# Sums for the down projection's left operands, made by VectorE and stored as seven operands

## The chip, the cores and the metric

One NeuronCore of one Trainium2 chip runs the whole program. The metric is the time of one execution on the device in microseconds (us). The engines are TensorE (PE in the profile, PEld its weight loads), VectorE (DVE), ScalarE (ACT), GpSimd (POOL) and SyncE (SP), whose queue issues nearly all transfers. Each engine runs its own instructions strictly in its own order and waits for others by semaphores.

## The reference

One layer of a decoder trunk on 1024 tokens of width 1024, in f32. The change concerns the feed-forward part alone:

```
h = rms_norm(x, ffn_norm_g)
x = x + (silu(h @ ffn_w_gate) * (h @ ffn_w_up)) @ ffn_w_down      # 1024 -> 2816 -> 1024
gate = sigmoid(rms_norm(x, ple_norm_g) @ ple_w_gate)
x = x + (p @ ple_w_proj) * gate
return rms_norm(x, final_norm_g)
```

Ahead of it stand the input projection, three token mixers and the output projection; nothing in them is changed.

## The kernel before

Matrices are kept transposed (features on the 128 partitions, tokens along the free dimension). Every f32 operand of a matmul is split in two: `split` (line 1037) makes the high part with a ScalarE cast (L1039) and the low part with a VectorE subtraction (`sub`, which all have line 267), and each product of 128x128 by 128x512 is three matmuls (high by high, high by low, low by high).

Both parts of the feed-forward use a fast 2x2 block multiplication: seven block products in place of eight, whose operands are sums and differences of the blocks a11 to a22 of the left matrix and b11 to b22 of the right one. In the order of use the seven left operands are: 5: a21+a22; 6: operand 5 minus a11; 3: a12 minus operand 6; 1: a11; 7: a11-a21; 4: a22; 2: a12.

**Feed-forward stage** (loop over `c`, 11 turns, lines 1278 to 1297). A turn computes 256 of the 2816 features by two objects of `Pair` (lines 1076 to 1134): n = 0 for the gate weights, n = 1 for the up weights. A Pair loads two 512 KB weight tiles (L1083), makes its sums on GpSimd (L1102 and L267), splits its seven operands and runs seven products of 12 matmuls (`prod`, L1050 to L1052) into three of the eight PSUM banks: `first` and `second` into bank a, `sixth` into b, `fifth` into c, and `rest` adds the other three. ScalarE copies partial results out of the banks. `quarters` (L1267, L1268) combines the banks and copies into four quarters on VectorE and GpSimd. For n = 0 these go into `act`, two tiles of 128x1024, and through Silu. For n = 1 they go into `up_` and are multiplied into `act` (L1295; quarters 1 and 3, which are a21 and a22 later, on GpSimd, the other two on VectorE), and both `act` tiles are written to `actd` in DRAM (L1297, 512 KB each). So a turn is 14 products, 168 matmuls.

**Down projection** (class `Down`, lines 1318 to 1351; loop at 1382 to 1408). It runs in four groups of three, three, three and two values of `c` (`DOWN`). A `Down` loads four 512 KB tiles, two of `actd` and two of `w_down` (L1326), and takes one tile `st` whose halves hold the running left sum `s` and right sum `t`. For each of the seven products in the order 5, 6, 3, 1, 7, 4, 2, `operands` makes the sums on GpSimd (four for the left: L1337 and three of L267; five for the right, L267), then splits left and right (ScalarE and VectorE). 36 matmuls per product in a group of three (L1406) go into the banks 0 to 3 or 4 to 7, and `drain` adds each bank to the result in SBUF on VectorE (L1316, L1369). The last group also loads and splits the next stage's weights (L1304 to L1308).

**What sets the order.** A planner (`Plan`) gives every tile one of 50 fixed slots of SBUF, 46 of them of 4 KB a partition, by program order and estimated times; a tile whose slot is still in use waits for its last reader. The compiler orders each engine's instructions by a simulated timeline, so that neighbouring parts of the program interleave; on the chip each engine then keeps that order, SyncE's queue included: a transfer that waits holds all transfers behind it.

Of the kernel before, what the change touches and what calls it, by code (L numbers as in the profile page):

```python
# [9 lines left out]
F32 = mybir.dt.float32  # L10
# [3 lines left out]
ALU = mybir.AluOpType  # L14
# [4 lines left out]
S = 1024  # L19
D = 1024  # L20
P = 128
# [5 lines left out]
MF = FF // P  # L27
# [191 lines left out]
def tile_block(ctx: ExitStack, tc: tile.TileContext, a: dict, out: bass.AP, plan: Plan):  # L219
    nc = tc.nc  # L220
# [7 lines left out]
    dram = ctx.enter_context(tc.tile_pool(name="dram", bufs=1, space=DRAM))  # L228
# [4 lines left out]
    def place(name, shape, dt):  # L233

        if dry:
            return big.tile(list(shape), dt, name=name, of=plan.add(4 * int(np.prod(shape[1:])), tc.clock))
        return big.tile(list(shape), dt, name=name, tag=f"s{plan.at[next(made)]}", bufs=1)

    def B(name, dt=F32, shape=(P, 1024)):
        return place(name, shape, dt)  # L240
# [7 lines left out]
    class Ring:  # L248


        def __init__(self, lo, hi):
            self.lo, self.hi, self.at = lo, hi, lo
# [10 lines left out]
    def f(ap):  # L263
        return ap.bitcast(F32)

    def sub(eng, o, i0, i1):
        return eng.tensor_tensor(out=o, in0=i0, in1=i1, op=ALU.subtract)  # L267
# [30 lines left out]
    def rstd_of(src, n, tag):  # L298

        r = SM(f"rs{tag}", src.shape)  # L300
        nc.gpsimd.tensor_scalar(out=r, in0=src, scalar1=1.0 / n, scalar2=EPS, op0=ALU.mult, op1=ALU.add)
        nc.gpsimd.tensor_tensor(out=r, in0=r, in1=mhalf[:, :src.shape[1]], op=ALU.pow)
        return r
# [413 lines left out]
    for t in range(NT):  # L717
# [4 lines left out]
        src = ps[:, :256].rearrange("p (g d) -> p g d", d=HD)  # L722
# [6 lines left out]
        if t > 2:  # L729
            pump(near, 1)  # L730
    nc.vector.tensor_tensor(out=gcmp, in0=gates.rearrange("p t (h b) -> p t h b", b=3)[:, :, :, 0],
                            in1=rowok.unsqueeze(2).to_broadcast([P, NT, H]), op=ALU.mult)
# [41 lines left out]
    for which in range(2):  # L774
# [4 lines left out]
        for u in range(2):  # L779
            for g in range(2):  # L780
                src = cv[g * 64:(g + 1) * 64, :].rearrange("p (n j) -> p j n", j=16)
                for q in range(2):
                    js = slice(q * 8, q * 8 + 8)
                    nc.vector.tensor_tensor(
                        out=X[q][u * 64:(u + 1) * 64, :, g * NCMP:(g + 1) * NCMP],
                        in0=src[:, js, u:u + NCMP],
                        in1=pos[g * 64:(g + 1) * 64, u, js].unsqueeze(2).to_broadcast([64, 8, NCMP]), op=ALU.add)
# [249 lines left out]
    def split(src):  # L1037
        o = B("op", F32R, (P, 2, 512))
        nc.scalar.copy(o[:, 0, :], src)  # L1039
        sub(nc.gpsimd if pool_lo[0] > 0 else nc.vector, o[:, 1, :], src, f(o[:, 0, :]))  # L1040
        pool_lo[0] -= 1
        return o

    def half(x, n):
        return x[:, n * 512:(n + 1) * 512]
# [91 lines left out]


    x1d = dram.tile([KT, P, S], F32, name="x1d")
    actd = dram.tile([MF, P, S], F32, name="actd")  # L1140
    xop, outs = {}, {}

    def out_half(m, hf, kts, first, last):
# [58 lines left out]
    for u in range(len(units) + LOOK):  # L1202
        ga = gb = iter(())
        if u < len(units):
            h, j = units[u]
# [25 lines left out]
    for m in range(KT):  # L1231
# [5 lines left out]
        if m == 4:  # L1237

            r = Right(raws[:4], [None] * 4)
# [3 lines left out]
    pairs = {}  # L1243
# [20 lines left out]
    def quarters(p, out):  # L1264

        rr = half(rbc1, 0), half(rbc1, 1)
        add = lambda eng, o, i0, i1: eng.tensor_tensor(out=o, in0=i0, in1=i1, op=ALU.add)  # L1267
        mult = lambda eng, o, i0, i1: eng.tensor_tensor(out=o, in0=i0, in1=i1, op=ALU.mult)  # L1268
        c11, c12, c21, c22 = out
        mult(nc.vector, c11, p.a, rr[0])  # L1270
        add(nc.vector, c12, p.c, p.p6)
        mult(nc.vector, c12, c12, rr[1])
        add(nc.vector, c21, p.b, p.p1)
        mult(nc.vector, c21, c21, rr[0])
        add(nc.gpsimd, c22, p.p67, p.p5)
        mult(nc.vector, c22, c22, rr[1])

    for c in range(MF // 2):
        for n in range(2):
            if (c, n) not in pairs:  # L1280
                pairs[c, n] = Pair(a["w_u" if n else "w_g"], 2 * c, r)
                pairs[c, n].first()
            p = pairs.pop((c, n))
            p.rest()
            if n == 0:
                act = [B("sg") for _ in range(2)]
                quarters(p, [half(g, i) for g in act for i in range(2)])
                for g in act:
                    nc.scalar.activation(g, g, AF.Silu)
            else:  # L1290
                up_ = [B("ws", F32, (P, 512)), p.p6, p.p1, p.p5]
                quarters(p, up_)
                for i, o in enumerate(up_):
                    g = half(act[i // 2], i % 2)
                    (nc.gpsimd if i in UPP else nc.vector).tensor_tensor(out=g, in0=o, in1=g, op=ALU.mult)  # L1295
                for i in range(2):
                    nc.sync.dma_start(out=actd[2 * c + i], in_=act[i])  # L1297


    wg = []  # L1300
# [17 lines left out]
    class Down:  # L1318


        def __init__(self, c):
            w = []
            for m in (2 * c, 2 * c + 1):
                for src in (actd[m], a["w_d"][m * P:(m + 1) * P, :]):
                    w.append(B("nat"))
                    nc.sync.dma_start(out=w[-1], in_=src)  # L1326
            self.a11, self.a21 = half(w[0], 0), half(w[0], 1)
            self.b11, self.b12 = half(w[1], 0), half(w[1], 1)
            self.a12, self.a22 = half(w[2], 0), half(w[2], 1)
            self.b21, self.b22 = half(w[3], 0), half(w[3], 1)  # L1330
            st = B("st", F32, (P, 2, 512))
            self.s, self.t = st[:, 0, :], st[:, 1, :]

        def operands(self, n):
            x = self
            if n == 5:
                nc.gpsimd.tensor_tensor(out=x.s, in0=x.a21, in1=x.a22, op=ALU.add)  # L1337
                sub(nc.gpsimd, x.t, x.b12, x.b11)
            if n == 6:
                sub(nc.gpsimd, x.s, x.s, x.a11)  # L1340
                sub(nc.gpsimd, x.t, x.b22, x.t)
            if n == 3:
                sub(nc.gpsimd, x.s, x.a12, x.s)
            if n == 7:
                sub(nc.gpsimd, x.a21, x.a11, x.a21)
                sub(nc.gpsimd, x.b12, x.b22, x.b12)
            if n == 4:
                sub(nc.gpsimd, x.t, x.b21, x.t)
            l, r = {5: (x.s, x.t), 6: (x.s, x.t), 3: (x.s, x.b22), 7: (x.a21, x.b12), 1: (x.a11, x.b11),
                    4: (x.a22, x.t), 2: (x.a12, x.b21)}[n]  # L1350
            return split(l), split(r)

    def acc(m, hf):
        return x2[hf][m % 4][:, m // 4, :]
# [27 lines left out]
    for q, cs in enumerate(DOWN):  # L1382
        ds = [Down(c) for c in cs]
        for n, g, start in ((5, 0, True), (6, 1, True), (3, 0, False), (1, 0, True), (7, 1, False), (4, 1, False),
                            (2, 0, False)):
            ops = [d.operands(n) for d in ds]
            if not x2:
                for hf in (1, 0):
                    x2.insert(0, [B("x2", F32, (P, 2, 512)) for _ in range(4)])
                    for m in range(KT):  # L1390
                        nc.sync.dma_start(out=acc(m, hf) if hf == 0 else x2[0][m % 4][:, m // 4, :],
                                          in_=half(x1d[m], hf))
# [9 lines left out]
            for t in range(4):  # L1402
                c = slice(t * P, (t + 1) * P)
# [26 lines left out]
    for i, t in enumerate(ORDER):  # L1430
        c = slice(t * P, (t + 1) * P)
        x, r3 = rows[i]
# [39 lines left out]
        r = rstd_of(ss, D, "r")  # L1472
# [64 lines left out]
def build(inputs):  # L1537
    import concourse.bacc as bacc

    nc = bacc.Bacc("TRN2", target_bir_lowering=False, num_devices=1)  # L1540
    arrays, aps = {}, {}
    for name, v in _layout({k: np.asarray(x) for k, x in inputs.items()}).items():
        v = np.ascontiguousarray(v)
        arrays[f"in_{name}"] = v
        aps[name] = nc.dram_tensor(f"in_{name}", v.shape, mybir.dt.from_np(v.dtype), kind="ExternalInput").ap()
    out = nc.dram_tensor("out_0", (S, D), F32, kind="ExternalOutput").ap()
    plan = Plan(SLOTS)
    tile_block(_Recorder(plan), aps, out, plan)
    plan.solve()
    with tile.TileContext(nc, schedule_with_timeline_sim=True) as tc:  # L1550
        tile_block(tc, aps, out, plan)
    return nc, arrays
# [8 lines left out]
```

## Time and profile before

| what | value |
|---|---|
| median of 3 runs | 1448.14 us (1444.1 to 1454.31) |
| the profiled execution's own time | 1443.36 us |
| its span, first to last instruction | 1441.6 us |
| busy: PE, DVE, ACT, POOL | 96%, 71%, 46%, 53% of the span |
| mean granted clock of TensorE | 0.988 of full speed |
| bytes moved | 118.36 MB, 82 GB/s |

The feed-forward stage lies from about 700 to 1077 us of the span and the down projection from about 1069 to 1316 us. A PE busy share is no measure of how full PE is, because matmuls overlap and the spans are modelled; the number of matmuls in a stretch is. In a timeline row the bracket says how long the engine was idle before, and who released it. "op" tiles are split operands, "nat" tiles are loaded as they are, "ws" and "st" hold sums, "cp" copies out of PSUM, "sg" is `act`.

### The profile page before, as it was taken

The page shows a single profiled execution, that of the slowest core. Times are in us where ns is not written, and L with a number is a line of the kernel's source. Part 1 is how long each engine was busy: PE and PEld are TensorE (multiplying, and loading weights), DVE is VectorE, ACT ScalarE, POOL GpSimd, SP SyncE. Part 2 cuts the span into 40 slices and gives each one's busy share as a digit, 9 for nine tenths or more (in the row PEclk, how much of TensorE's full clock was granted, in tenths as well). Part 3 has the DMA queues.
Part 4 walks back from the last instruction along what each step waited for, and adds up shares of the span by engine and source line. Part 5 has one row for each costly group of instructions (what it writes and reads, how often), then busy time and mean ns, then how long its engine had stood idle before and what let it go on. Part 6 is the DMA issues. An engine that isn't in the chain of part 4 may idle for free.

```text
span 1441.6 us, 19394 instructions
## 1 busy us (share of the span) xinstructions
PE 1387.6 (96%) x7080; PEld 1163.3 (81%) x7080; DVE 1028.8 (71%) x1738; ACT 665.6 (46%) x1290; POOL 765.6 (53%) x724
## 2 busy tenths in 40 slices
PE   8999999999999989999989999999997999999998
PEld 6898777889999978887768888888775877887886
DVE  3896548459999875678666666656679999987533
ACT  7321522348888874554333333333334343444632
POOL 3850433447887761045656665656687848514111
PEclk9999999999999999999999999999997999999999
DMA  9201012500000023521212222222282331321111
GB/s 350 74 16 49 16 57 80 165 0 5 9 5 5 5 92 126 181 73 45 88 73 75 86 88 88 88 73 88 65 298 93 132 139 38 131 74 62 66 41 44
DMA packets 40782, 118.36 MB, mean 82 GB/s; under 512 B 4532, under 2 KB 9326, under 8 KB 40686
## 3 DMA queue, kind: packets, MB, share of 16 engines
q1 hardware_dynamic: 40542, 117.11, 23.6%
q8 instruction: 55, 0.90, 0.3%
q14 instruction: 41, 0.34, 0.1%
q10 hardware_dynamic: 144, 0.01, 0.0%
HBM read 94.03 MB, written 23.08 MB: 81 GB/s over the span
## 4 chain that ended last, share of the span: by engine, by line
PE 52%; DVE 17%; POOL 12%; DMA 7%; issue 6%; ACT 5%; SPq 0%; POOLq 0%; DVEq 0%; ACTq 0%
DVE op L267 10%; PE banks L1406 6%; POOL ws L267 4%; PE banks L966 3%; PE banks L371 3%; PE banks L372 3%; PE banks L368 3%; ACT op L1039 3%; PE banks L1010 2%; PE banks L1011 2%; DMA nat<-in_w_u 2%; PE banks L906 2%; PE banks L1456 2%; PE banks L1457 2%; PE banks L1458 2%
## 5 line engine op out<-in xcount | busy, mean ns | idle before, releaser
L1050 PE MATMUL banks<-op 128*128 128x512 f32 x616 | 237.1, 393 | 8.2 <-ACT op L1039 4.2
L1051 PE MATMUL banks<-op 128*128 128x512 f32 x616 | 240.5, 391 | 0.7 <-DVE op L267 0.7
L1406 PE MATMUL banks<-op 128*128 128x512 f32 x924 | 222.6, 402 | 18.4 <-DVE x L1316 6.6
L1052 PE MATMUL banks<-op 128*128 128x512 f32 x616 | 238.9, 392 | 0.6 <-DVE op L267 0.4
L1406 PEld LDWEIGHTS banks<-op 128*128 128x128 f32 x924 | 178.1, 194 | 62.6 <-DVE x L1316 9.4
L267 DVE TENSOR_TENSOR op<-nat,op 128x512 fp32r<-128x512 f32 x174 | 162.0, 949 | 57.1 <-ACT op L1039 55.5
L1039 ACT CAST op<-nat 128x512 fp32r<-128x512 f32 x178 | 106.3, 620 | 179.1 <-DVE op L267 64.7
L1050 PEld LDWEIGHTS banks<-op 128*128 128x128 f32 x616 | 116.0, 188 | 37.3 <-ACT op L1039 5.1
L267 DVE TENSOR_TENSOR op<-ws,op 128x512 fp32r<-128x512 f32 x88 | 89.9, 1026 | 73.4 <-ACT op L1039 71.3
L1052 PEld LDWEIGHTS banks<-op 128*128 128x128 f32 x616 | 115.9, 188 | 27.3 <-DVE op L267 2.7
L1051 PEld LDWEIGHTS banks<-op 128*128 128x128 f32 x616 | 116.1, 188 | 24.9 <-DVE op L267 1.1
L921 POOL TENSOR_SCALAR p<-p,sums,gates 128x640 f32<-128x640 f32 (+7 forms) x128 | 100.4, 795 | 36.4 <-DVE sums L917 26.8
L1039 ACT CAST op<-ws 128x512 fp32r<-128x512 f32 x88 | 54.3, 620 | 101.1 <-POOL ws L267 74.7
L912 ACT ACTIVATE p<-p,mn 128x640 f32<-128x640 f32 (+7 forms) x128 | 94.8, 742 | 10.2 <-DVE mn L909 10.1
L368 PE MATMUL banks<-hT,whi 128*128 128x512 f32 x208 | 83.9, 404 | 6.8 <-ACT hT L324 6.2
L371 PE MATMUL banks<-hT,whi 128*128 128x512 f32 x208 | 83.4, 401 | 0.5 <-DVE hT L325 0.5
L372 PE MATMUL banks<-hT,wlo 128*128 128x512 f32 x208 | 82.0, 396 | 0.0
L267 DVE TENSOR_TENSOR op<-st,op 128x512 fp32r<-128x512 f32 x66 | 77.9, 1199 | 5.6 <-ACT op L1039 5.4
L1039 ACT CAST op<-st 128x512 fp32r<-128x512 f32 x66 | 39.8, 619 | 77.8 <-POOL st L267 48.3
L966 PE MATMUL banks<-cst,p 128*128 128x128 f32 x448 | 71.2, 274 | 2.0 <-DVE pt L267 1.0
L906 PE MATMUL banks<-k,qst 128*128 128x512 f32 (+2 forms) x192 | 68.0, 360 | 1.0 <-POOL qst L267 0.5
L267 DVE TENSOR_TENSOR pt<-banks,pt 128x512 fp32r<-128x512 f32 (+1 forms) x114 | 64.2, 571 | 5.9 <-ACT pt L977 4.9
(297 smaller groups left out, 3459.8 us busy)
## 6 DMA issues: line engine op xcount, KB each, us to landing
nat<-in_w_g SPq DMA_DIRECT2D x22, 512.0 KB, 3.3
nat<-in_w_u SPq DMA_DIRECT2D x22, 512.0 KB, 3.2
actd<-sg SPq DMA_DIRECT2D x22, 512.0 KB, 2.9
nat<-in_w_d SPq DMA_DIRECT2D x22, 512.0 KB, 5.3
nat<-actd SPq DMA_DIRECT2D x22, 512.0 KB, 4.6
nat<-in_w_t SPq DMA_DIRECT2D x13, 512.0 KB, 4.2
xT<-in_xT SPq DMA_DIRECT2D x16, 256.0 KB, 5.8
x<-in_x SPq DMA_DIRECT2D x8, 512.0 KB, 8.0
```

What stands on the lines that cost most here:

```text
L267: return eng.tensor_tensor(out=o, in0=i0, in1=i1, op=ALU.subtract)
L368: r = mm(o, hi[:, w], x[:, 0, :], start=kt == 0, stop=False)
L371: mm(o, hi[:, w], x[:, 1, :], start=False, stop=False)
L372: mm(o, lo_[:, w], x[:, 0, :], start=False, stop=kt == KT - 1)
L906: mark("pe", mm(ps[:, :max(w, 256)], q, kdup[br][g][:, k], start=True, stop=False))
L921: nc.gpsimd.tensor_scalar(out=ps_out[br][:, :n], in0=ps_out[br][:, :n], scalar1=sums[:, br:br + 1], scalar2=gates[:, qb, 3 * head(h) + 1 + ...
L966: nc.tensor.transpose(ps[:, (2 * m + e) * P:(2 * m + e + 1) * P], blk(e, kb, br, ka), ident)
L1039: nc.scalar.copy(o[:, 0, :], src)
L1050: mm(ps, w[:, 0, c], x[k][:, 0, :], start=start and k == 0, stop=False, skip_group_check=True)
L1051: mm(ps, w[:, 0, c], x[k][:, 1, :], start=False, stop=False, skip_group_check=True)
L1052: mm(ps, w[:, 1, c], x[k][:, 0, :], start=False, stop=k == 3, skip_group_check=True)
L1406: mm(groups[g][t], r[:, v, c], l[:, u, :], start=start and (i, u, v) == (0, 0, 0), stop=i == len(ops) - 1 and u == 1, skip_group_check=True)
```

## The change

`actd` becomes seven blocks of 128x512 for each `c`, one for each left operand in the order 5, 6, 3, 1, 7, 4, 2. In the feed-forward stage, behind the multiplications of n = 1, VectorE makes operands 5, 6, 3 and 7 in four instructions (5 and 6 in a new tile `sa`, 3 in the first tile of `up_`, 7 in place of a21), and five transfers write the seven blocks: 512 KB for 5 and 6, 256 KB for 3, 512 KB for 1 and 7, 256 KB for 4 and for 2.

`Down` loads the two weight tiles, operands 5 and 6 as one tile, and operand 2 into the half of `st` that `s` had; operands 3 and 1 are loaded when product 5's operands are made, 7 and 4 when product 3's are. GpSimd makes only the right sums.

In the last turn (c = 10) both Pairs are set up ahead: `first` of both, `sixth` of both, `fifth` of both, and only then the `rest` of each.

```
-    actd = dram.tile([MF, P, S], F32, name="actd")
+    actd = dram.tile([MF // 2, 7, P, 512], F32, name="actd")

     for c in range(MF // 2):
+        if c == MF // 2 - 1:
+            for n in range(2):
+                pairs[c, n] = Pair(a["w_u" if n else "w_g"], 2 * c, r)
+                pairs[c, n].first()
+            for n in range(2):
+                pairs[c, n].sixth()
+            for n in range(2):
+                pairs[c, n].fifth()
...
-                for i in range(2):
-                    nc.sync.dma_start(out=actd[2 * c + i], in_=act[i])
+                a11, a21, a12, a22 = (half(g, i) for g in act for i in range(2))
+                sa = B("sa", F32, (P, 2, 512))
+                s5, s6, s3 = sa[:, 0, :], sa[:, 1, :], up_[0]
+                nc.vector.tensor_tensor(out=s5, in0=a21, in1=a22, op=ALU.add)
+                sub(nc.vector, s6, s5, a11)
+                sub(nc.vector, s3, a12, s6)
+                sub(nc.vector, a21, a11, a21)
+                nc.sync.dma_start(out=actd[c, 0:2].rearrange("i p j -> p i j"), in_=sa)
+                nc.sync.dma_start(out=actd[c, 2], in_=s3)
+                nc.sync.dma_start(out=actd[c, 3:5].rearrange("i p j -> p i j"), in_=act[0].rearrange("p (i j) -> p i j", i=2))
+                nc.sync.dma_start(out=actd[c, 5], in_=a22)
+                nc.sync.dma_start(out=actd[c, 6], in_=a12)
...
         def __init__(self, c):
+            self.c, self.a = c, {}
             w = []
             for m in (2 * c, 2 * c + 1):
-                for src in (actd[m], a["w_d"][m * P:(m + 1) * P, :]):
-                    w.append(B("nat"))
-                    nc.sync.dma_start(out=w[-1], in_=src)
...
+                w.append(B("nat"))
+                nc.sync.dma_start(out=w[-1], in_=a["w_d"][m * P:(m + 1) * P, :])
+            self.b11, self.b12, self.b21, self.b22 = (half(x, i) for x in w for i in range(2))
+            self.load(5, 6)
             st = B("st", F32, (P, 2, 512))
-            self.s, self.t = st[:, 0, :], st[:, 1, :]
+            self.t, self.a[2] = st[:, 0, :], st[:, 1, :]
+            nc.sync.dma_start(out=self.a[2], in_=actd[c, 6])
+
+        def load(self, n0, n1):
+            i = (5, 6, 3, 1, 7, 4).index(n0)
+            w = B("nat", F32, (P, 2, 512))
+            nc.sync.dma_start(out=w, in_=actd[self.c, i:i + 2].rearrange("i p j -> p i j"))
+            self.a[n0], self.a[n1] = w[:, 0, :], w[:, 1, :]

             if n == 5:
-                nc.gpsimd.tensor_tensor(out=x.s, in0=x.a21, in1=x.a22, op=ALU.add)
+                x.load(3, 1)
                 sub(nc.gpsimd, x.t, x.b12, x.b11)
             if n == 6:
-                sub(nc.gpsimd, x.s, x.s, x.a11)
                 sub(nc.gpsimd, x.t, x.b22, x.t)
             if n == 3:
-                sub(nc.gpsimd, x.s, x.a12, x.s)
+                x.load(7, 4)
             if n == 7:
-                sub(nc.gpsimd, x.a21, x.a11, x.a21)
                 sub(nc.gpsimd, x.b12, x.b22, x.b12)
```

## Rows read from the trace of the kernel before

**Rows 1.** the page: span; busy us (share), instructions of each engine

```profile
span 1441.6 us, 19394 instructions
...
PE 1387.6 (96%) x7080; PEld 1163.3 (81%) x7080; DVE 1028.8 (71%) x1738; ACT 665.6 (46%) x1290; POOL 765.6 (53%) x724
```

**Rows 2.** stages: length, busy us (instructions) per engine, clock, DMA share, GB/s

```profile
738.00:1044.00 306.00, 305.17 (x1332) 250.24 (x1333) 192.96 (x222) 115.57 (x192) 184.68 (x126) 0.99 0.23 81
...
1069.00:1120.00 51.00, 38.59 (x132) 28.78 (x131) 47.33 (x48) 20.79 (x37) 40.40 (x24) 0.83 0.43 150
1120.00:1160.00 40.00, 38.45 (x169) 31.20 (x168) 37.60 (x43) 13.60 (x24) 37.56 (x24) 1.00 0.31 106
1160.00:1200.00 40.00, 40.00 (x178) 33.12 (x177) 39.12 (x53) 16.79 (x29) 20.40 (x14) 1.00 0.44 158
1200.00:1250.00 50.00, 47.68 (x203) 38.87 (x202) 48.23 (x62) 21.75 (x38) 28.54 (x18) 0.97 0.21 74
1250.00:1316.00 66.00, 63.86 (x277) 50.99 (x275) 61.83 (x77) 25.74 (x38) 30.39 (x19) 1.00 0.19 64
```

**Rows 3.** PE timeline, late feed-forward stage: start, us, instruction

```profile
1060.06 0.39 PE L1051 MATMUL banks<-op 128*128 128x512 f32 x1
...
1065.72 0.39 PE L1052 MATMUL banks<-op 128*128 128x512 f32 x1
```

**Rows 4.** PE timeline, start of the down projection

```profile
1090.00 6.51 PE L1406 MATMUL banks<-op 128*128 128x512 f32 x15 [3.38 <-DVE op L267]
...
1101.93 8.23 PE L1406 MATMUL banks<-op 128*128 128x512 f32 x26 [1.41 <-DVE x L1316]
```

**Rows 5.** VectorE timeline, start of the down projection

```profile
1081.44 1.77 DVE L267 TENSOR_TENSOR op<-nat,op 128x512 fp32r<-128x512 f32 x1
...
1101.80 2.97 DVE L267 TENSOR_TENSOR op<-nat,op 128x512 fp32r<-128x512 f32 x4
```

**Rows 6.** GpSimd timeline, the same stretch

```profile
1055.91 1.30 POOL L1134 TENSOR_TENSOR cp<-cp 128x512 f32<-128x512 f32 x1
...
1080.93 1.73 POOL L267 TENSOR_TENSOR st<-st,nat 128x512 f32<-128x512 f32 x1
```

**Rows 7.** groups of instructions, GpSimd, 1048 to 1316 us

```profile
L267 POOL TENSOR_TENSOR st<-nat,st 128x512 f32<-128x512 f32 x33 | 57.1, 1746 | 7.6 <-DVE op L267 7.6
...
L1337 POOL TENSOR_TENSOR st<-nat 128x512 f32<-128x512 f32 x11 | 18.4, 1675 | 10.5 <-PE banks L1406 6.4 <-DMA nat<-actd 4.1
```

**Rows 8.** chain of waits, 845 to 930 us: shares; start, us, what

```profile
by line: DMA nat<-in_w_u 14.6%; POOL ws L267 14.1%; DVE op L267 12.5%; POOL sg L1295 10.4%; issue 10.2%; ACT op L1039 8.1%; POOL cp L1133 5.8%; DVE sg L1268 5.6%; DMA nat<-in_w_g 3.7%; POOL cp L1134 3.4%; POOL cp L1267 3.1%; DVE cp L1268 2.
...
884.01 2.94 POOL sg L1295 x2
...
887.38 4.24 DMA nat<-in_w_u
```

**Rows 9.** VectorE timeline, the same turn

```profile
890.89 0.68 DVE L1268 TENSOR_TENSOR sg<-banks,rbc 128x512 f32<-128x512 f32 x1
893.73 2.81 DVE L267 TENSOR_TENSOR op<-ws,op 128x512 fp32r<-128x512 f32 x2 [2.16 <-ACT op L1039]
898.38 0.69 DVE L267 TENSOR_TENSOR op<-ws,op 128x512 fp32r<-128x512 f32 x1 [1.84 <-ACT op L1039]
```

**Rows 10.** SyncE queue timeline, the same turn

```profile
848.58 0.33 SPq L1297 DMA_DIRECT2D actd<-sg  x1
849.00 0.39 SPq L1083 DMA_DIRECT2D nat<-in_w_u  x1
...
857.14 10.81 SPq L1083 DMA_DIRECT2D nat<-in_w_g  x2
...
886.97 0.33 SPq L1297 DMA_DIRECT2D actd<-sg  x1
```

**Rows 11.** SyncE queue timeline, start of the down projection

```profile
1091.10 0.32 SPq L1297 DMA_DIRECT2D actd<-sg  x1
...
1112.57 0.32 SPq L1297 DMA_DIRECT2D actd<-sg  x1
```

More of the change, by code (lines that the diff above doesn't have):

```diff
@@ L1321, in __init__ @@
         def __init__(self, c):
+            self.c, self.a = c, {}
             w = []
             for m in (2 * c, 2 * c + 1):
-                for src in (actd[m], a["w_d"][m * P:(m + 1) * P, :]):
-                    w.append(B("nat"))
-                    nc.sync.dma_start(out=w[-1], in_=src)
[L1327 to L1330, printed above, removed]
-            st = B("st", F32, (P, 2, 512))
-            self.s, self.t = st[:, 0, :], st[:, 1, :]
+                w.append(B("nat"))
+                nc.sync.dma_start(out=w[-1], in_=a["w_d"][m * P:(m + 1) * P, :])
+            self.b11, self.b12, self.b21, self.b22 = (half(x, i) for x in w for i in range(2))
+            self.load(5, 6)
+            st = B("st", F32, (P, 2, 512))
+            self.t, self.a[2] = st[:, 0, :], st[:, 1, :]
[5 more added lines that the diff above has]
+            self.a[n0], self.a[n1] = w[:, 0, :], w[:, 1, :]
         def operands(self, n):
@@ L1348, in operands @@
                 sub(nc.gpsimd, x.t, x.b21, x.t)
-            l, r = {5: (x.s, x.t), 6: (x.s, x.t), 3: (x.s, x.b22), 7: (x.a21, x.b12), 1: (x.a11, x.b11),
-                    4: (x.a22, x.t), 2: (x.a12, x.b21)}[n]
-            return split(l), split(r)
+            return split(x.a.pop(n)), split({3: x.b22, 1: x.b11, 7: x.b12, 2: x.b21}.get(n, x.t))
     def acc(m, hf):
```

## The prediction

> **What bounds the kernel now.** I read the page first: PE is busy 96% of a span of 1441.6 us, VectorE 71%, GpSimd 53% [rows 1]. The reader should not stop at that 96%, since overlapping spans hide gaps; I count matmuls instead. In the dense end of the feed-forward stage 25 matmuls start in 1065.72 - 1060.06 = 5.66 us, so one costs 0.2264 us at full clock [rows 3]. The stage table then gives each stretch's loss as its length less matmuls x 0.2264 [rows 2]:
>
> - 738 to 1044 (feed-forward): 306 - 1332 x 0.2264 = 4.4 us lost.
> - 1069 to 1120 (end of feed-forward, first group of the down projection): 51 - 132 x 0.2264 = 21.1 us lost.
> - 1120 to 1316 (the rest of it): 40 + 40 + 50 + 66 = 196 us for 169 + 178 + 203 + 277 = 827 matmuls, 187.2 us; 8.8 us lost.
>
> So the feed-forward stage runs at PE's pace, and what an edit can win back is about 30 us between 1069 and 1316. In that stage the same table shows who is late: VectorE is busy 47.3 + 37.6 + 39.1 + 48.2 + 61.8 = 234 of 247 us, 95%. In the feed-forward stretch it is busy 193 of 306 us, 63%; 14 us in each of its eight turns are free. In the first part of the down projection PE's gaps end with VectorE, and after the gaps it also runs at a lower clock: 15 matmuls take 6.51 us there, 0.43 each, with a granted clock of 0.83 over the stretch [rows 2, 4], a mean between the two levels of 2.4 and 1.2 GHz.
>
> **Why VectorE is late there.** With GpSimd idle, four low parts take 2.97 us, one starting each 0.60 us to 0.76 us; with GpSimd running the same instruction takes 1.77 us, and its successor starts 1.70 us later [rows 5]. GpSimd's instruction stretches as well, from 1.30 to 1.73 us [rows 6]. In one place, then, a GpSimd instruction alongside costs VectorE 1.70 - 0.60 = 1.1 us. Over the stage the price is lower, because VectorE's additions from PSUM keep their pace: 283 VectorE instructions x 0.60 = 170 us, busy 234, so 64 us over 99 GpSimd instructions, 0.65 us each; in the first stretch (47.3 - 48 x 0.60) / 24 = 0.77 us [rows 2].
>
> **The change, part by part.**
>
> *Left sums leave GpSimd.* Each of 11 values of c loses four GpSimd instructions in the down projection (L1337 and three of L267), 44 in all, of 1.68 to 1.75 us [rows 7]: some 74 us of GpSimd and, by 0.65 us each, 29 us of VectorE (0.5 to 1.1: 22 to 48 us). VectorE's 234 us become about 205, under the 217 us that the stage's 959 matmuls need. In the first stretch some 11 of the 24 GpSimd instructions go: 11 x 0.77 = 8.5 us of VectorE, which paces that stretch; I add 2.5 us for matmuls that return to full clock (15 of them cost 15 x (0.43 - 0.226) = 3 us too much [rows 4]). Gain 11 us. Of the 8.8 us behind 1120 I count 6 back; VectorE stays near full and PE keeps some waits. Sum: 17 us, of 30. Bounds: 2 us, if the lost time sits in the order of the queues and not in VectorE's amount of work; 28 us, if nearly all of it goes. What is late next is PE.
>
> *Four sums for VectorE in each turn of the feed-forward stage.* Alone 4 x 0.60 = 2.4 us, beside GpSimd 4 x 1.70 = 6.8 us [rows 5]; I take 4. Cover is the 14 us a turn in which VectorE is idle. Ahead of 893.73 and 898.38 it idles 2.16 and 1.84 us, right where the sums would go [rows 9]. They must wait for GpSimd's two products, which end at 884.01 + 2.94 = 886.95 [rows 8]; behind them in VectorE's order stand the low parts of the next Pair, which PE waits for. Without cover it is 4 us a turn.
>
> *Five writes instead of two, three more read issues.* An issue takes 0.33 us of SyncE [rows 10]: 1 us more per turn. 3 more blocks of 256 KB a turn are 0.8 MB, some 20 GB/s over 38 us where 81 are moved at a DMA share of 0.23 [rows 2]; hidden. The writes wait for VectorE's sums, and what stands behind them on SyncE waits too: now an up-weight load follows the first write at once, 849.00 after 848.58, and the gate-weight load comes at 857.14 [rows 10]. Sums begun at 849 end by 853 at 4 us, and five issues end by 855, ahead of 857. I expect the up-weight load to be ordered ahead of the writes. In the down projection the operands now come in three loads spread over the group; before, all first-group loads had been issued ahead of the last turn's writes, which SyncE reached at 1091.10 and 1112.57 [rows 11]. I count 0 for all of this, with bounds of -4 us (the 4.4 us of the stretch return because the load no longer hangs on a write) and +20 us (2 us a turn over ten turns).
>
> *One more 4 KB tile a turn, and the last turn's new order.* The slot of `sa` comes back only when its write has read it; a weight load may wait for it. The new order moves sums and splits of the last Pair ahead by some products, takes VectorE work out of the stretch from 1069 and adds four sums to it (2.4 to 6.8 us, off PE's path as long as group 1 does not need them). No row prices these; by the nearest, 0.76 us of VectorE each way, I take +1 us for both, bounds -4 and +8.
>
> **Sum.** -17 + 0 + 1 = -16 us. The profiled execution's own time is 1443.4 us, 1.8 more than its span and 4.8 below the median of the runs, 1448.1. 1443.4 - 16 = 1427.4 on its scale; on the median's, 1432.
>
> **A rule weighed.** Rows 5 show a VectorE instruction with two SBUF inputs slowed by a GpSimd one beside it, and rows 6 the reverse. The Trainium skill, "SBUF — State Buffer", section "Who interferes with whom", says that such a pair shares one read interface under an exclusive lock: whichever starts second stands still until the other ends. That speaks against the new sums as well as for the old ones' removal: each could hold a GpSimd instruction for a full VectorE instruction, by an estimate from that page some 0.6 us, 2.4 us a turn. The trace has 0.43 us (1.73 - 1.30). By the rule alone the feed-forward stage would lose 24 us more over ten turns if GpSimd sets its pace; it is the rival next below.
>
> **Rivals.**
>
> *Slower: the feed-forward loop lengthens.* The chain through two turns is made of transfers, GpSimd, VectorE and ScalarE, with no PE among its larger shares; in it stand GpSimd's two products (2.94 us), the write's issue, then the up-weight load (4.24 us) [rows 8]. From write to write it takes 886.97 - 848.58 = 38.39 us [rows 10], where PE needs 168 x 0.2264 = 38.04. The loop of VectorE, GpSimd, SyncE and slots is thus as long as PE's work, with no slack. If the sums fall into it (the load behind the first write, or low parts behind the sums), a turn grows by 3.3 us: four sums of 0.60 plus two GpSimd stretches of 0.43. Over ten turns 33 us, less 17: 1448 + 16 = 1464 us. It decides from 1.7 us a turn. For it: the chain. Against: VectorE's idle 14 us a turn, and the freedom to order the load ahead.
>
> *No change: VectorE is relieved, but PE waits as long.* The freed time is lost to late operands: loads of 3, 1, 7 and 4 wait for a slot or behind the last turn's writes. Then 6 us of the 17 come, and the feed-forward stage costs 2: 1444 us. For it: SyncE's hold-ups in the first group [rows 11]. Against: two products of 36 matmuls, 16 us, lie between each load's place and its use.
>
> *More: nearly all the loss goes.* 28 us in the down projection and 4 in the feed-forward stage: 1416 us. Against it: VectorE would still be busy 205 of 217 us.
>
> **How the numbers follow.** Forecast 0.47, own range 1422 to 1438; no change 0.24 (1438 to 1455); more 0.11 (1412 to 1422); slower 0.18 (1453 to 1475). A measurement of this kernel tells about 1%, 14.5 us, from no change; the bounds are 1433.7 and 1462.6. Three quarters of the forecast (0.35) and all of the third case make faster 0.46. Five sixths of the slower case make slower 0.15. The rest, 0.39, is the same. The range 1417 to 1466 leaves out half of the third case and a third of the slower one, some 0.12 in all, and reaches nearly to the sum of the bounds.
>
> **What would show it.** Right: 1069 to 1120 holds clearly more matmuls and a clock near 1; VectorE's low parts from `st` and `nat` in the down projection have shorter means; GpSimd has 44 instructions fewer there; a feed-forward turn stays near 38 us from write to write. Wrong in the feed-forward part: turns of 40 us or more, PE idle released by low parts. Wrong in the down projection: PE or ScalarE idle released by the loads from `actd`. A time above 1450 would say that the loop, not VectorE's amount of work, was the thing to watch.

## The result and the profile after

The changed kernel took 1428.4 us in the median (1426.5 to 1431.7, 4 runs), the kernel before 1448.8 us beside it: a ratio of 0.986, 95% interval 0.9821 to 0.990. Measured again later, the same pair gave 0.9903 (0.9886 to 0.992). The change is faster, by some 1.2%; the two measurements differ by 0.4%, and their intervals just overlap. Forecast was 1432 us.

The page after, to be held against [rows 1]:

```profile
span 1424.7 us, 19476 instructions
...
PE 1380.7 (97%) x7080; PEld 1159.6 (81%) x7080; DVE 1034.4 (73%) x1782; ACT 662.6 (47%) x1290; POOL 692.8 (49%) x680
```

The span is 16.9 us shorter. GpSimd has 44 instructions fewer and 73 us less to do, VectorE 44 more and only 6 us more. PE does the same 7080 matmuls. The stages after, in the columns of [rows 2]:

```profile
738.00:1044.00 306.00, 302.62 (x1315) 245.02 (x1314) 219.44 (x249) 111.84 (x188) 177.42 (x124) 1.00 0.28 99
1069.00:1120.00 51.00, 45.42 (x183) 35.77 (x182) 47.34 (x67) 23.50 (x42) 26.50 (x15) 0.93 0.63 221
1120.00:1160.00 40.00, 37.68 (x166) 30.89 (x165) 39.95 (x56) 19.21 (x36) 17.66 (x11) 1.00 0.38 140
1160.00:1200.00 40.00, 40.00 (x178) 33.10 (x177) 33.65 (x47) 14.24 (x25) 17.78 (x12) 1.00 0.56 204
1200.00:1250.00 50.00, 50.00 (x222) 41.41 (x221) 43.97 (x62) 22.74 (x39) 11.90 (x8) 1.00 0.40 137
1250.00:1299.00 49.00, 48.52 (x213) 39.54 (x212) 45.12 (x60) 19.16 (x27) 13.77 (x8) 1.00 0.19 65
```

Read as before, length less matmuls x 0.2264 us: the stretch from 1069 to 1120 holds 183 matmuls where it held 132, 51 more or 11.5 us of PE's work, and its clock rose from 0.83 to 0.93. From 1120 to the end the loss is 179 - 779 x 0.2264 = 2.6 us, where it was 8.8. So of 29.9 us that the stage lost, 12.2 are left. VectorE is busy 210 of 230 us, where it was 234 of 247. In the first stretch it is as busy as ever, 47.3 of 51 us, but gets through 67 instructions in that time, not 48: it still sets the pace there, at a higher one. The PE timeline of the changed kernel shows where its gaps stop, to be held against [rows 4]:

```profile
1089.15 2.20 PE L1426 MATMUL banks<-op 128*128 128x512 f32 x5 [2.81 <-DVE op L267]
1092.04 51.28 PE L1426 MATMUL banks<-op 128*128 128x512 f32 x216 [0.69 <-DVE op L267]
1145.63 148.97 PE L1426 MATMUL banks<-op 128*128 128x512 f32 x656 [2.32 <-DVE x L1335]
```

From 1145.6 on, 656 matmuls run with no gap that the trace shows, and the chain that ended last goes through PE alone for 105 us. Low parts that VectorE makes in the down projection, first before, then after (form, count, busy us, mean ns):

```profile
L267 DVE TENSOR_TENSOR op<-nat,op 128x512 fp32r<-128x512 f32 x89 | 79.2, 913 | 0.9
L267 DVE TENSOR_TENSOR op<-st,op 128x512 fp32r<-128x512 f32 x66 | 77.9, 1199 | 5.6 <-ACT op L1039 5.4
```

```profile
L267 DVE TENSOR_TENSOR op<-nat,op 128x512 fp32r<-128x512 f32 x111 | 90.1, 843 | 4.5 <-ACT op L1039 4.2
...
L267 DVE TENSOR_TENSOR op<-st,op 128x512 fp32r<-128x512 f32 x43 | 38.5, 909 | 2.1 <-ACT op L1039 1.9
```

Low parts of sums in `st` fell from 1199 to 909 ns in the mean, those of loaded tiles from 913 to 843 ns: the neighbour that slowed them is active about half as often. In the five stretches from 1069 us on GpSimd has 54 instructions where it had 99 [rows 2].

The feed-forward stage went the other way. From 738 to 1044 it holds 1315 matmuls where it held 1332, 17 fewer or 3.8 us. SyncE's queue shows what moved. The first fence is the kernel before, where one up-weight load of the next turn (the second follows the write at 848.58 in [rows 10]) stands ahead of the writes; the second is the changed kernel, in which L1315 is the write of operand 4 (a22), L1312 that of 5 and 6, L1313 that of 3:

```profile
772.86 0.33 SPq L1297 DMA_DIRECT2D actd<-sg  x1
...
843.04 0.33 SPq L1083 DMA_DIRECT2D nat<-in_w_u  x1
...
1003.69 0.33 SPq L1297 DMA_DIRECT2D actd<-sg  x1
```

```profile
767.09 0.33 SPq L1315 DMA_DIRECT2D actd<-sg  x1
...
886.16 0.33 SPq L1315 DMA_DIRECT2D actd<-sg  x1
886.59 0.87 SPq L1083 DMA_DIRECT2D nat<-in_w_u  x2
888.09 0.38 SPq L1312 DMA_DIRECT2D actd<-sa  x1
...
890.74 1.25 SPq L1313 DMA_DIRECT2D actd<-ws  x1
...
1003.77 0.33 SPq L1315 DMA_DIRECT2D actd<-sg  x1
```

From 767.09 to 1003.77 are six turns, 39.45 us each. Six turns of the kernel before, from 772.86 to 1003.69, took 38.47 each, and PE needs 38.04. The compiler put the write of a22 first, ahead of *both* up-weight loads of the next turn; before, one of the two stood ahead of the writes. Both loads now wait until GpSimd has made a22. The longest waits of that queue (what waited, for whom, us in all, times, the longest) and the chain of waits say the same:

```profile
SPq L1315 <- POOL sg L1303: 106.5, 8, 14.2
```

```profile
884.47 1.68 POOL sg L1303
...
886.16 0.33 SPq L1315
...
886.59 3.72 DMA nat<-in_w_u
```

The chain of [rows 8] is still there, product, write, up-weight load, with the load now 0.4 us behind the write for both tiles. How much of the longer turn is the order and how much the sums, the experiments tell. What the stage lost in its turns it had won at its start. Stages of the kernel before, then after:

```profile
636.00:700.00 64.00, 61.45 (x267) 47.95 (x266) 52.95 (x63) 29.32 (x49) 32.84 (x33) 1.00 0.16 58
700.00:738.00 38.00, 32.35 (x141) 25.86 (x140) 24.02 (x26) 13.34 (x23) 21.76 (x16) 1.00 0.20 69
```

```profile
636.00:700.00 64.00, 58.53 (x252) 46.38 (x251) 54.43 (x67) 29.97 (x50) 37.30 (x34) 0.98 0.20 70
700.00:738.00 38.00, 38.00 (x168) 31.40 (x168) 23.94 (x30) 13.45 (x22) 21.97 (x16) 0.99 0.28 97
```

By 738 us the changed kernel is 267 + 141 = 408 against 252 + 168 = 420 matmuls, 12 ahead. At 1069 us it is 3 matmuls behind, 0.7 us. The whole difference in span, 16.9 us, lies in the down projection.

### The profile page after: what moved, and what is told of

Read it like the earlier page. It is cut to its first block, busy times and chain, and to the rows that moved or that the text cites. A ratio compares the mean times of both kernels' runs of the same rounds, so it can differ in the third digit from the quotient of the medians.

```text
span 1424.7 us, 19476 instructions
## 1 busy us (share of the span) xinstructions
PE 1380.7 (97%) x7080; PEld 1159.6 (81%) x7080; DVE 1034.4 (73%) x1782; ACT 662.6 (47%) x1290; POOL 692.8 (49%) x680
## 4 chain that ended last, share of the span: by engine, by line
PE 58%; DVE 16%; POOL 9%; ACT 6%; issue 6%; DMA 4%; SPq 0%; POOLq 0%; DVEq 0%; ACTq 0%
DVE op L267 8%; PE banks L1426 7%; POOL ws L267 4%; PE banks L966 3%; PE banks L371 3%; PE banks L372 3%; PE banks L368 3%; ACT op L1039 3%; PE banks L1010 2%; PE banks L1011 2%; PE banks L906 2%; PE banks L1476 2%; PE banks L1477 2%; PE banks L1478 2%; PE banks L907 2%
## 5 line engine op out<-in xcount | busy, mean ns | idle before, releaser
L1039 ACT CAST op<-nat 128x512 fp32r<-128x512 f32 x200 | 117.7, 619 | 174.3 <-DVE op L267 64.0
L267 DVE TENSOR_TENSOR op<-nat,op 128x512 fp32r<-128x512 f32 x196 | 164.9, 864 | 38.5 <-ACT op L1039 37.9
L267 DVE TENSOR_TENSOR op<-ws,op 128x512 fp32r<-128x512 f32 x88 | 99.5, 1131 | 73.4 <-ACT op L1039 69.6
L1335 DVE TENSOR_TENSOR x<-banks,x 128x512 f32<-128x512 f32 x96 | 63.4, 679 | 5.5 <-PE banks L1426 5.4
L267 POOL TENSOR_TENSOR st<-nat 128x512 f32<-128x512 f32 x11 | 21.1, 1919 | 90.7 <-DMA nat<-in_w_d 84.2
```

## The experiments

**Only GpSimd's left sums go.** The kernel before without them; the down projection then computes something else, because operands 5, 6, 3 and 7 are the plain blocks a21, a22, a12 and a21.

```
-                nc.gpsimd.tensor_tensor(out=x.s, in0=x.a21, in1=x.a22, op=ALU.add)
-                sub(nc.gpsimd, x.s, x.s, x.a11)
-                sub(nc.gpsimd, x.s, x.a12, x.s)
-                sub(nc.gpsimd, x.a21, x.a11, x.a21)
...
-            l, r = {5: (x.s, x.t), 6: (x.s, x.t), 3: (x.s, x.b22), 7: (x.a21, x.b12), 1: (x.a11, x.b11),
+            l, r = {5: (x.a21, x.t), 6: (x.a22, x.t), 3: (x.a12, x.b22), 7: (x.a21, x.b12), 1: (x.a11, x.b11),
```

> The kernel before, with GpSimd's four left sums per value of c left out of the down projection: the products 5, 6, 3 and 7 take the blocks a21, a22, a12 and a21 as they are, so the down projection's result is another one. Nothing is added in the feed-forward stage, nothing changes in the transfers. Theory A (VectorE's amount of work: each GpSimd instruction beside it costs it about 0.65 us): the whole gain of the down projection comes, 21 us, without the feed-forward stage's cost: 1427 us (1420 to 1433), VectorE's busy time from 1069 us on some 29 us less. Theory B (the gain came from the last turn's new order or from where the loads stand): 1440 to 1449 us.

Measured: 1425.9 us, ratio 0.985 (0.9832 to 0.9867), 21.6 us less than the kernel before beside it. The first stretch of its down projection (columns of [rows 2]), and its page, to be held against [rows 1]:

```profile
1069.00:1120.00 51.00, 46.28 (x196) 37.50 (x195) 46.72 (x60) 24.22 (x42) 27.19 (x18) 0.97 0.65 239
```

```profile
PE 1383.2 (97%) x7080; PEld 1163.8 (82%) x7080; DVE 997.7 (70%) x1738; ACT 665.3 (47%) x1290; POOL 688.9 (48%) x680
```

Over the whole run VectorE executes 1738 instructions in both kernels and is busy 997.7 us against 1028.8, 31.1 less. (Two later versions of the kernel before, with another order of the same work, have 1030.8 and 1034.5, so a few us of this are scatter.) Taking away 44 instructions of *another* engine shortened VectorE's work by about 0.7 us for each, and with nothing else changed the whole gain of the change is there. In this run's trace the feed-forward stage starts 6.3 us later than before (642.3 against 636.0), so stretches at fixed times do not hold quite the same work. Theory A stands, theory B falls.

**The same sums, on VectorE, in the same place.**

```
-                nc.gpsimd.tensor_tensor(out=x.s, in0=x.a21, in1=x.a22, op=ALU.add)
+                nc.vector.tensor_tensor(out=x.s, in0=x.a21, in1=x.a22, op=ALU.add)
```

and the three subtractions likewise.

> The kernel before, with the four left sums per value of c made by VectorE in place of GpSimd, still in the down projection. Theory A (amount of work on VectorE): 44 instructions of 0.60 us or more are added, 26 us, and 44 x 0.65 = 29 us of slowing go: no change, 1442 to 1452 us. Theory C (what was late was GpSimd's chain of sums, 1.7 us each, ahead of the splits): the chain is shorter now, and most of the gain comes, 1425 to 1437 us.

Measured: 1444.1 us, ratio 0.9974 (0.9958 to 0.9989). Two stretches and the page:

```profile
1069.00:1120.00 51.00, 43.22 (x172) 33.73 (x171) 44.26 (x61) 23.61 (x42) 29.08 (x15) 0.93 0.49 178
1120.00:1320.00 200.00, 190.05 (x807) 151.72 (x805) 194.57 (x272) 76.34 (x128) 64.41 (x40) 0.98 0.28 97
```

```profile
PE 1390.6 (96%) x7080; PEld 1163.8 (81%) x7080; DVE 1026.6 (71%) x1782; ACT 664.2 (46%) x1290; POOL 696.5 (48%) x680
```

With 44 instructions more than in the run without the sums VectorE is busy 1026.6 us over the whole run, 28.9 more, 0.66 us for each. A sum costs VectorE about as much when GpSimd makes it (0.7) as when it makes it itself (0.66); GpSimd saved it nothing that can be measured. Theory C falls as an account of the whole time, which is nearly that of the kernel before. For the first stretch it is partly right. Counted from the last matmul of the feed-forward stage, the next 42.1 us hold 99 matmuls in the kernel before, 139 here and 159 without the sums. Here the time won is lost again behind it: 1120 to 1320 loses 200 - 807 x 0.2264 = 17.3 us, where the kernel before lost 8.8, with VectorE busy 194.6 of 200. For the whole time it counts that the sums leave the stage, not which engine makes them there.

**The last turn's order, taken out and put in alone.** The first edit removes this block from the changed kernel, the second adds it to the kernel before.

```
-        if c == MF // 2 - 1:
-            for n in range(2):
-                pairs[c, n] = Pair(a["w_u" if n else "w_g"], 2 * c, r)
-                pairs[c, n].first()
-            for n in range(2):
-                pairs[c, n].sixth()
-            for n in range(2):
-                pairs[c, n].fifth()
```

> The changed kernel without the new order of the last turn (c = 10 is set up like every other turn). Theory A (the gain is VectorE's relief in the down projection): most of the gain stays, 1428 to 1436 us. Theory B (the new order of the last turn brings the start of the down projection its work earlier, and that is the gain): 1438 to 1449 us.

> The kernel before with the new order of the last turn alone. Theory A: within 5 us of the kernel before, 1443 to 1453 us. Theory B: a large part of the gain, 1428 to 1438 us.

Measured: 1431.7 us without it, ratio 0.9887 (0.9872 to 0.9902), between the changed kernel's own two ratios; and 1448.1 us with it alone, ratio 0.9994 (0.9981 to 1.0007). Theory B falls a second time. The new order by itself does nothing that can be measured.

**The sums of the feed-forward stage on GpSimd.**

```
-                nc.vector.tensor_tensor(out=s5, in0=a21, in1=a22, op=ALU.add)
+                nc.gpsimd.tensor_tensor(out=s5, in0=a21, in1=a22, op=ALU.add)
```

and the three subtractions likewise.

> The changed kernel with the four sums of the feed-forward stage made by GpSimd in place of VectorE. If idle time covers them as it mostly did on VectorE (GpSimd is idle some 15 us a turn): 1426 to 1432 us. If the loop of a turn, in which GpSimd's instructions stand in a row, has no slack: four of 1.3 to 1.7 us lengthen a turn by 2 to 5 us and the time is 1445 to 1475 us.

Measured: 1434.9 us, ratio 0.9917 (0.9894 to 0.994); turns from write to write 39.0 us. Between the two expectations, and not to be told from the changed kernel's second ratio. The order of the queue was not held here: in four of seven turns one up-weight load stands ahead of the write of a22 again (in one of them at 838.13, the write at 842.88). With that order, GpSimd's sums cost the stage no more than VectorE's do in the changed kernel; which engine is better under the same order is not shown.

**The changed kernel without the sums.** Blocks are written from `act` as they stand, so the down projection computes something else.

```
-                sa = B("sa", F32, (P, 2, 512))
-                s5, s6, s3 = sa[:, 0, :], sa[:, 1, :], up_[0]
-                nc.vector.tensor_tensor(out=s5, in0=a21, in1=a22, op=ALU.add)
-                sub(nc.vector, s6, s5, a11)
-                sub(nc.vector, s3, a12, s6)
-                sub(nc.vector, a21, a11, a21)
-                nc.sync.dma_start(out=actd[c, 0:2].rearrange("i p j -> p i j"), in_=sa)
-                nc.sync.dma_start(out=actd[c, 2], in_=s3)
+                nc.sync.dma_start(out=actd[c, 0:2].rearrange("i p j -> p i j"), in_=act[0].rearrange("p (i j) -> p i j", i=2))
+                nc.sync.dma_start(out=actd[c, 2], in_=a12)
```

> The changed kernel without VectorE's four sums and without the tile sa: the seven blocks are written from act as it stands (blocks a11 and a21 twice, a12 twice), so the down projection's result is another one; the five writes, the loads and the last turn's order stay. Theory A: the down projection's gain stays, and what the sums cost in the feed-forward stage (a turn of 39.4 us in place of 38.4) comes back: 1419 to 1424 us. Rival (the turn is longer because the up-weight loads wait behind the writes on SyncE, whatever is computed): turns stay near 39.4 us, 1427 to 1431 us.

Measured: 1437.4 us, ratio 0.9925 (0.9905 to 0.9944). Less work, and not faster: the ratio lies above both of the changed kernel's, and its interval overlaps that of the second. Both expectations missed. The queue of SyncE in that run:

```profile
774.85 0.33 SPq L1309 DMA_DIRECT2D actd<-sg  x1
...
856.37 0.33 SPq L1309 DMA_DIRECT2D actd<-sg  x1
857.62 0.38 SPq L1306 DMA_DIRECT2D actd<-sg  x1
858.05 0.46 SPq L1308 DMA_DIRECT2D actd<-sg  x1
858.61 0.82 SPq L1083 DMA_DIRECT2D nat<-in_w_u  x1
...
1020.00 0.33 SPq L1309 DMA_DIRECT2D actd<-sg  x1
```

Six turns from 774.85 to 1020.00, 40.86 us each. Without the sums to wait for, the compiler placed the other writes earlier too, and now *three* of them, 512 KB, 512 KB and 256 KB (L1309 is a22, L1306 and L1308 are taken from `act[0]`), stand ahead of an up-weight load. The edit had changed the order of the queue along with the work, so it could not tell the two apart. The next runs hold the order.

**Both up-weight loads ahead of the writes.** Two ways. First by a merged write: operands 2 and 4 go out in one transfer from the second `act` tile, which is ready later, and the compiler then puts both loads ahead of it.

```
-                nc.sync.dma_start(out=actd[c, 5], in_=a22)
-                nc.sync.dma_start(out=actd[c, 6], in_=a12)
+                nc.sync.dma_start(out=actd[c, 5:7].rearrange("i p j -> p i j"), in_=act[1].rearrange("p (i j) -> p i j", i=2))
...
-            nc.sync.dma_start(out=self.a[2], in_=actd[c, 6])
+            nc.sync.dma_start(out=self.a[2], in_=actd[c, 5])
...
-            nc.sync.dma_start(out=w, in_=actd[self.c, i:i + 2].rearrange("i p j -> p i j"))
+            nc.sync.dma_start(out=w, in_=(actd[self.c, 4:7:2] if n0 == 7 else actd[self.c, i:i + 2]).rearrange("i p j -> p i j"))
```

> The changed kernel with operands 2 and 4 written by one transfer from the second act tile, which is complete only after its other quarter, in place of two: four writes a turn, and in SyncE's order both up-weight loads now stand ahead of all writes of the turn. If the turn is longer because the up-weight loads hang on the write of a22 behind GpSimd's product: a turn falls from 39.4 to some 38.2 us, over nine turns 11 us, 1416 to 1423 us. If the four sums' time on VectorE and beside GpSimd is what lengthens it: no change, 1426 to 1431 us.

> The kernel with four writes a turn once more, with more rounds: if it is a version that beats the changed kernel, its ratio to the kernel before stays at 0.980 to 0.985 (1420 to 1427 us) and its turns at 38.1 us; if the earlier run's 0.9825 was chance, 0.986 to 0.990 like the two runs of the changed kernel.

Measured: 1423.8 us, ratio 0.9825 (0.9806 to 0.9845), and again 1424.7 us, ratio 0.9839 (0.982 to 0.9857). The second run's queue:

```profile
767.79 0.81 SPq L1083 DMA_DIRECT2D nat<-in_w_u  x2
...
882.25 0.80 SPq L1083 DMA_DIRECT2D nat<-in_w_u  x2
886.63 0.38 SPq L1315 DMA_DIRECT2D actd<-sg  x1
...
996.27 0.81 SPq L1083 DMA_DIRECT2D nat<-in_w_u  x2
```

Six turns from 767.79 to 996.27, 38.08 us each: PE's pace, with the four sums in place. The turns are those expected; the time is not quite, 1423.8 us where 1416 to 1423 was expected. These are the lowest ratios here. Both intervals lie below the changed kernel's second one and overlap the first; this version and the changed kernel were not timed side by side.

Then by an order dependency: the five writes are stated behind the last up-weight load of the next turn, once with the sums and once without, beside the changed kernel itself.

```
+    def store(load):
+        for o, g in held:
+            ins = nc.sync.dma_start(out=o, in_=g)
+            if not dry and load is not None:
+                tc.add_manual_dep(ins.ins, load.ins.name,
+                                  mybir.DependencyInfo(mybir.DependencyClass.NoSync, mybir.DependencyReason.DATA))
+        held.clear()
```

> The changed kernel with its five writes of a turn issued behind both up-weight loads of the next turn on SyncE. Loop theory: turns fall from 39.4 to about 38.1 us, as in the run with four writes, 1418 to 1426 us. Rival (the merged write helped there, not the order): 1427 to 1431 us.

> The same order of the writes, and VectorE's four sums and the tile sa left out as in the earlier run without sums (the blocks are written from act as it stands, so the down projection's result is another one). Loop theory: once no load hangs on a write, turns are at PE's pace with and without the sums: within 3 us of the run with the same order and the sums, and far from the 1437 us of the earlier run without sums. Rival (the sums themselves cost the feed-forward stage 4 us or more): 4 us or more faster than with the sums; or, if leaving out sums is bad for another reason, 1435 us or more again.

> The changed kernel as it is, on the same chip as the three runs with another order of the writes: 1426 to 1432 us, turns of about 39.4 us from write to write.

Measured: 1428.5 us with the order and the sums, ratio 0.9865 (0.984 to 0.989); 1425.5 us with the order and without sums, 0.9847 (0.9825 to 0.9868); 1434.1 us for the changed kernel itself, 0.9903 (0.9886 to 0.992), where 1426 to 1432 was expected. In the queue with the sums and then without them:

```profile
770.99 0.82 SPq L1083 DMA_DIRECT2D nat<-in_w_u  x2
...
1003.89 0.82 SPq L1083 DMA_DIRECT2D nat<-in_w_u  x2
```

```profile
771.96 5.35 SPq L1083 DMA_DIRECT2D nat<-in_w_u  x2
...
1001.76 5.35 SPq L1083 DMA_DIRECT2D nat<-in_w_u  x2
```

Six turns are 232.90 and 229.80 us, 38.8 and 38.3 us each, against 39.5 us for the changed kernel beside them. The two runs without sums differ in the order alone: turns of 40.9 and of 38.3 us, ratios of 0.9925 and 0.9847, whose intervals lie apart. So the order by itself does cost time. With the order held, leaving out the sums no longer makes it slower; it saves 0.5 us a turn, 3 us in the time, within the intervals of both. With the sums in place the order brought 0.7 us a turn and not the 1.3 that the loop theory had, and the time, 1428.5 us, is in the range of its rival. So order and sums share the longer turn, and with the merged write even the sums are covered; why that write does better than the stated order is open.

**The same order for the kernel before.** Its two writes are stated behind the up-weight loads in the same manner.

```
-                for i in range(2):
-                    nc.sync.dma_start(out=actd[2 * c + i], in_=act[i])
+                held += [(2 * c + i, act[i]) for i in range(2)]
...
                 pairs[c, n] = Pair(a["w_u" if n else "w_g"], 2 * c, r)
+                if n == 1:
+                    for m, g in held:
+                        store(m, g, pairs[c, n].load)
+                    held = []
```

> The kernel before, with the two act writes of a turn issued behind both up-weight loads of the next turn on SyncE (an order dependency, no wait added). Loop theory (a turn is as long as the loop write, up-weight load, sums makes it): turns fall from 38.5 to about 38.1 us, PE's pace, and the time by 3 to 10 us: 1438 to 1446 us. Rival (SyncE's order does not matter, the loop closes elsewhere): 1446 to 1451 us.

Measured: 1447.3 us, ratio 0.9998 (0.9986 to 1.0011). The turns did fall: seven of them, from load to load, from 768.58 to 1034.91, 38.05 us each.

```profile
768.58 5.35 SPq L1083 DMA_DIRECT2D nat<-in_w_u  x2
...
1034.91 5.35 SPq L1083 DMA_DIRECT2D nat<-in_w_u  x2
```

The time did not. The low-by-high matmuls of the feed-forward stage and the matmuls of the down projection (first to last start in us) tell where the stages end, for the kernel before and for this run:

```profile
L1052 PE MATMUL banks<-op x616: 387/389/799, 636.5 to 1077.7; 128*128 128x512 f32 x154
L1406 PE MATMUL banks<-op x924: 387/389/796, 1069.7 to 1315.7; 128*128 128x512 f32 x185
```

```profile
L1052 PE MATMUL banks<-op x616: 387/389/800, 638.9 to 1075.7; 128*128 128x512 f32 x154
L1419 PE MATMUL banks<-op x924: 387/389/796, 1065.0 to 1319.7; 128*128 128x512 f32 x185
```

The stage ended 2 us earlier though it began 2.4 us later, and the down projection's last matmul came at 1319.7 where it came at 1315.7. What the turns gave was taken back behind them. There VectorE is full (busy 189.7 of the 200 us from 1120 in this run), and the waits of the down projection's products that end with VectorE add up to 23.2 us where they were 12.9. That VectorE's load is the cause fits these waits; no run isolates it. The changed kernel and the version with four writes, at the second measurement, show a milder loss:

```profile
L1052 PE MATMUL banks<-op x616: 387/389/799, 636.9 to 1081.2; 128*128 128x512 f32 x154
```

```profile
L1052 PE MATMUL banks<-op x616: 387/389/799, 637.9 to 1070.3; 128*128 128x512 f32 x154
```

The feed-forward stage ends 10.9 us earlier with four writes, and the down projection 2.6 us earlier (1296.3 against 1298.9 us). Here the loss lies between the two stages. The down projection takes as long from its first matmul to its last (225.8 against 225.4 us), but its first comes only 3.0 us earlier (1070.5 against 1073.5): in the changed kernel it had started before the other stage ended. What holds it there is open.

## Why the prediction was right

- **VectorE, loaded by its neighbour, sets the down projection's pace.** Right for the whole time, and shown: removing GpSimd's sums alone gave the gain, moving them to VectorE gave nearly none. Priced at 0.65 us of VectorE per GpSimd instruction with bounds of 0.5 and 1.1; the run without the sums has about 0.7. VectorE was to fall from 234 to 205 us in the stage; it fell to 210. For the first stretch the account leaves something out: GpSimd is busy 40.4 of 51 us there [rows 2], and with the sums on VectorE 40 of the 60 matmuls that their removal wins were won in the 42.1 us behind the feed-forward stage.
- **The first stretch gives 11 us, the rest 6.** 11.5 and 8.8 - 2.6 = 6.2 us. That closeness is partly luck: the 2.5 us for the clock and the 6 of 8.8 were choices between wide bounds.
- **The sums are covered in the feed-forward stage.** The total was right, 0.7 us at 1069 us; the step was not, and that the total came out is luck. I expected the up-weight loads to be ordered ahead of the writes. With the second `act` tile written in two transfers, the compiler made a22's the first and put both loads behind it. A turn grew by 1 us, within the bound of 2. That the start of the stage gave 12 matmuls back was not foreseen. It comes with the sums: over the first 102 us of the stage the seven traces of versions that make them there hold 415 to 429 matmuls, the seven others 405 to 409. How the sums bring it about is open.
- **The slower rival** had the right place, the loop of product, write and load, and the wrong price: 1 us a turn, not 3.3. From 738 to 1005 most of the sums stay out of GpSimd's way, 0.69 us for operand 5 and 0.68 for operands 6 and 7 in the mean, 1.00 for operand 3, since GpSimd stands idle for some 5 us behind its product. With four writes (second run, 738 to 1044) they do not, 1.53 us for operand 3 and 0.96 for operand 7, and the turn is at PE's pace all the same: VectorE is busy only 240 of the 306 us to 1044. That bears on the rule weighed there (the Trainium skill, "SBUF — State Buffer", "Who interferes with whom"): it matters where instructions of the two engines overlap in time. In the down projection they do, and there the runs agree with the rule in kind; the price per instruction, about 0.7 us of VectorE, is about half of the 1.3 us that a GpSimd instruction takes at its fastest [rows 6].
- **One more tile and the last turn's order, +1 us.** The order alone: ratio 0.9994. The tile alone was not tried.
- **The other two rivals.** "No change" expected late operands. SyncE's waits in the down projection exist, but in the first stretch PE's gaps still end with VectorE's low parts. "More" needed VectorE out of the way; from 1145.6 us it is, but the first stretch kept 9.6 of its 21.1 us, and VectorE is as full there as before.

## What to carry to other kernels

Where instructions of two engines slow each other and one of the engines is full, count the other's instructions as the full one's work: moving a sum between the two gained next to nothing here, moving it into a stage where the full engine has idle time gained nearly all of it. Where a store and the next loads go through one queue, look at which stands first, in the timeline of that queue and after every edit; leaving out work can move a store ahead of a load and cost more than the work did. A stage that is sped up ahead of a stage with a full engine can give its gain back, as the kernel before did under the new order: read the end of the next stage too, and not the turns alone.

## What had not been expected of the hardware

A GpSimd addition or subtraction of 128x512 f32 takes VectorE about 0.7 us of progress when VectorE is full, against 0.66 us for making the same sum itself. And the same two kernels, compared on two occasions, gave ratios of 0.986 and 0.9903. In the two traces of the changed kernel 4.7 of the 7.8 us between them lie ahead of the feed-forward stage, whose first matmul starts at 636.4 and at 641.1 us, in a part that the change leaves alone. For differences of half a per cent between versions, both have to run side by side, and a stage is best timed from its own start.
